# A depthwise convolution woven into a matmul stream: the last far products behind the next gate, one reduce for the cached tokens, low parts and mean later

## The chip, the core and the metric

The kernel runs on one core of a Trainium2 chip. Its engines work side by side, each through its own queue in order: TensorE (PE in the rows, PEld for its weight loads), VectorE (DVE), ScalarE (ACT), GpSimd (POOL) and SyncE (SP), which issues the DMAs here. Semaphores tie them together. The metric is the device time in microseconds, the median of several runs.

## What is computed

One inference step of a two-layer decoder trunk, for 256 new positions of one prompt and 8 sampled tokens (264 columns together), all in float32. Layer 0 mixes tokens with a Conformer convolution, layer 1 with an HGRN2 recurrence; each layer ends in a convolutional feed-forward net. The change lies in the Conformer convolution:

```python
h = x @ w_pw1 + b_pw1
a, gt = jnp.split(h, 2, axis=-1)
u = a * jax.nn.sigmoid(gt)
c, new_buf = causal_depthwise_conv(u, buf, w_dw, b_dw)
c = jax.nn.silu(layernorm(c, ln_g, ln_b))
return c @ w_pw2 + b_pw2, new_buf
```

D_MODEL and D_CONV are 2048, CONV_WIDTH is 31: each channel is convolved with 31 taps over time. For the sampled tokens the 30 older inputs come from a cached state.

## The kernel before

Channels lie on the 128 partitions, so x and every 2048-channel tensor are 16 tiles of 128 x 264. Weights are read in tiles of 128 output channels (1 MB each); one such tile is one *slot* (`slot`), 16 k-steps on TensorE. A weight tile is used in one of two ways (`step`): *native* float32, one matmul per k-step (L184), or *split* into a high part (a cast on ScalarE, L145, `wh`) and a low part (a subtraction on VectorE, L157, `wl`), three matmuls per k-step (L187 to L189), which then also need the activations' high and low parts (`high_parts`, `low_parts`, L275 for the low ones).

The order of work is written out by hand. `slot` first emits the matmuls of its weight tile and then takes its *turn*: three lists of functions, *first*, *early* and *late*, with the casts of coming weights between the first two and their subtractions between the last two. `later(n, f)` puts f into the n-th turn from now. Each engine works through what has been emitted for it in that order.

In the first convolution slots alternate: slot 2i makes a's channel tile i, slot 2i+1 its gate tile. The first 16 and three gate tiles are native, the gate tiles of i >= 3 split. The work on tile i is put into the turns of slots 2i+2 and 2i+3:

- `sigmoid` (L387, ScalarE), then `glu` (L395, VectorE), which makes the tile's gated input `u`; a copy of its end (`ulast`, L397).
- `begin_sums`: ScalarE starts two sums in PSUM, `even` (L413) and `odd` (L414), and one in SBUF, `far` (L419, from the negative of a mean m0; for the first two tiles GpSimd sets it to zero).
- `taps`: 15 instructions on VectorE (L404) that add one tap each to `even` or `odd`.
- `products`: the 14 far taps, in seven pairs. ScalarE multiplies (L435, into `two` for the first pair and `more` for the others, two buffers of `more`), GpSimd adds each pair into `two` (L437) and at the end both halves of `two` into `far` (L443).
- `end_sums`: VectorE adds even and far (L454), the sampled tokens (L455) and odd (L457) into `c`. It stands at the head of the next tile's turn, behind that tile's gate and ahead of its taps.
- `square` and `summed`: running sums of c and its square for the layer norm (L367 on ScalarE, four instructions at L380 on VectorE: `dq` in PSUM, `dsum` and `qsum` for the 8 tokens in SBUF).

For the last tile (15) 13 of the taps are matmuls with diagonal matrices (`diagonals`, L468 on ScalarE; `diagonal_taps`, L474). `centre` takes the column mean of tile 0's c by a matmul with ones (L479), ScalarE scales it into m0 (L481), and it is subtracted from all later sums, so that the squares lose less precision; tiles 0 and 1, which come before it, are corrected afterwards (`catch_up`, L486). `conv_state` multiplies the cached inputs by their taps (L347) and sums them over the 30 positions by halving (L352, L355) into `csum`.

PSUM has three banks of the kind `pt` for the weight slots and the mean. A slot's bank is free again when the tile's sigmoid (gate) or `glu` (a) has read it. The mean's bank is free when L481 has read it.

In time: slots 0 to 5 run without split weights; `conv_state` and `high_parts` stand late in the turn of slot 2, `low_parts` early in that of slot 3, `centre` late in that of slot 5, the catch-ups of tiles 0 and 1 in those of slots 6 and 9, `diagonals` late in that of slot 28. Behind the last tile's sums come the layer norm's statistics, the second pointwise convolution, the feed-forward net, the HGRN2 layer and the second feed-forward net.

Of the kernel before, what the change touches and what calls it, by code (L numbers as in the profile page):

```python
# [49 lines left out]
TAPS, TAPS_LAST = (8, 17, CW), (7, 14, 18)  # L50
# [15 lines left out]
def kernel(ctx: ExitStack, tc: tile.TileContext, a: dict):  # L66
# [255 lines left out]
    with ExitStack() as ph:  # L322
# [23 lines left out]
        def conv_state():  # L346
            vec.tensor_tensor(out=cstate, in0=cstate, in1=wall[:, :, : CW - 1].unsqueeze(3).to_broadcast((P, KT, CW - 1, NB)),  # L347
                              op=ALU.mult)
            n = CW - 1
            while n > 1:  # L350
                half = n // 2
                vec.tensor_tensor(out=cstate[:, :, :half, :], in0=cstate[:, :, :half, :],  # L352
                                  in1=cstate[:, :, half : 2 * half, :], op=ALU.add)
                if n % 2:
                    vec.tensor_tensor(out=cstate[:, :, 0, :] if half > 1 else csum, in0=cstate[:, :, 0, :], in1=cstate[:, :, n - 1, :], op=ALU.add)  # L355
                n = half
            vec.tensor_tensor(out=csum, in0=csum, in1=par[:, COL["b_dw"] : COL["b_dw"] + KT].unsqueeze(2).to_broadcast((P, KT, NB)),
                              op=ALU.add)

        c, m = [], {}  # L360
# [8 lines left out]
        def summed(i):  # L369
            sq = m.pop(("sq", i))  # L370
            if i == 0:
                both = ps.tile([P, 2, SEQ], F32, tag="dq", name="dq", bufs=1)
                for r, z in enumerate("dq"):
                    m[z] = both[:, r, :], gp.tile([P, T], F32, tag=z + "sum", name=z + "sum")
            for z, t in zip("dq", (c[i], sq)):
                for own, cols in (m[z][0], slice(0, SEQ)), (m[z][1][:, SEQ:], slice(SEQ, T)):
# [31 lines left out]
        def begin_sums(i):  # L408
            u, last = m[i], i == KT - 1
            odd_from, top, end = TAPS_LAST if last else TAPS  # L410
# [5 lines left out]
            if i < 2:  # L416
# [5 lines left out]
            m["two", i] = gp.tile([P, 2, SEQ - TAPS_LAST[1]], F32, tag="two", name=f"two{i}")[:, :, : SEQ - top]  # L422
# [53 lines left out]
        def centre():  # L476
# [5 lines left out]
            later_tiles = csum[:, 2:, :]  # L482
            vec.tensor_tensor(out=later_tiles, in0=later_tiles, in1=m["m0"][:, SEQ:].unsqueeze(1).to_broadcast((P, KT - 2, NB)), op=ALU.subtract)
# [5 lines left out]
        def collected():  # L489
            for z in "dq":  # L490
                act.copy(m[z][1][:, :SEQ], m[z][0])
                m[z] = m[z][1]
# [15 lines left out]
        def low_parts():  # L508
            xhl[:] = [low(k, xg[k], xhl[k], "xg") for k in range(KT)]
# [4 lines left out]
        later(3, low_parts)  # L514
        for i in range(KT):
# [8 lines left out]
            if 0 < i < KT - 1:  # L524
                later(0, lambda i=i: end_sums(i - 1))
            if i == KT - 1:
                later(0, diagonal_taps)
                later(0, lambda i=i: (products(i, CW), taps(i, CW), end_sums(i), square(i)), last=True)
                continue
            later(0, lambda i=i: products(i, 2), first=True)  # L530
            later(0, lambda i=i: (products(i, 2), taps(i, 8)))
            later(1, lambda i=i: (products(i, CW), taps(i, CW)))
            if i == KT - 2:
                later(1, lambda i=i: (end_sums(i), square(i), summed(i), collected()), last=True)
                continue
            if i < 2:
                later(4 + i, lambda i=i: catch_up(i), last=True)
                later(5 + i, lambda i=i: summed(i))
            else:
                later(3, lambda i=i: square(i), first=True)  # L540
                later(3, lambda i=i: summed(i), last=True)
            if i == 0:
                later(3, centre, last=True)
            if i == KT - 3:
                later(0, diagonals, last=True)
# [646 lines left out]
```

## Time and profile before

| what | value |
|---|---|
| median of 3 runs (lowest to highest) | 2481.79 us (2481.58 to 2483.23) |
| the profiled execution's own time | 2483.45 us |
| its span, first to last instruction | 2481.7 us |
| mean granted TensorE clock | 0.990 |
| TensorE matmul, weight load busy | 2425.1 us (98%), 2381.4 us (96%) |
| VectorE, ScalarE, GpSimd busy | 1725.5 us (70%), 1249.9 us (50%), 160.8 us (6%) |
| first matmul of the first convolution | 7.57 us |
| gate of tile 0, of tile 15 (L395 starts) | 29.93 us, 259.13 us |
| first matmul of the second pointwise convolution | 276.80 us |

A row of the timeline or the chain gives the start in us, the length in us, engine, line, operation, output and inputs, shapes and a count; in brackets stands how long the engine had been idle before it, and what it waited for. A row of waits reads: engine, waiting line, what it waited for, us in total, times, (in some) the longest. A row of the stretches gives its bounds and length, then busy us (and instructions) of PE, PEld, DVE, ACT and POOL, then the granted clock, the DMA engines' busy share and GB/s. A row of the groups gives the line, the operation with shapes, a count, and behind the bar the sum in us and the mean of one in ns. A row of one line's instructions gives the shortest, median and longest length in ns. Lengths of neighbouring instructions of an engine can overlap by a little, so the step from start to start is used where one follows the other.

### The profile page before, as it was taken

How to read it: one execution, taken by the hardware profiler on the slowest of the kernel's cores; microseconds unless marked ns; L12 is line 12 of the kernel's file. 1: busy time of each engine (PE TensorE's matmuls, PEld its weight loads, DVE VectorE, ACT ScalarE, POOL GpSimd, SP SyncE). 2: the span in 40 equal slices, each digit the busy share in tenths (PEclk: the TensorE clock that was granted, in tenths of full speed). 3: DMA queues.
4: the chain of work that ended last, by engine and by line, in shares of the span. 5: the costliest groups of instructions: out<-in, count | busy, mean ns of one | idle time of the engine just before them, and what ended most of it. 6: DMA issues, size and time to landing. Idle time of an engine off the chain costs nothing.

```text
span 2481.7 us, 49276 instructions
## 1 busy us (share of the span) xinstructions
PE 2425.1 (98%) x20910; PEld 2381.4 (96%) x20910; DVE 1725.5 (70%) x2922; ACT 1249.9 (50%) x2112; POOL 160.8 (6%) x132
## 2 busy tenths in 40 slices
PE   7898799999999999999999999999999999999998
PEld 6898699999999999999999999999999999999998
DVE  8888857676566566657877877857767557656655
ACT  4667644444344344445766666544444444434434
POOL 2776100000000000000000000000000000000000
PEclk9999899999999999999999999999999999999999
DMA  7343255555455465455666555555555455455453
GB/s 266 136 161 145 102 189 190 185 174 175 164 204 182 156 207 180 165 178 200 217 214 221 204 203 213 187 196 197 178 187 173 157 207 177 162 199 183 164 179 126
DMA packets 78141, 453.09 MB, mean 183 GB/s; under 512 B 8544, under 2 KB 13024, under 8 KB 39008
## 3 DMA queue, kind: packets, MB, share of 16 engines
q1 hardware_dynamic: 77920, 449.94, 52.4%
q8 instruction: 164, 2.69, 0.4%
q14 instruction: 57, 0.47, 0.0%
HBM read 436.31 MB, written 15.50 MB: 182 GB/s over the span
## 4 chain that ended last, share of the span: by engine, by line
PE 78%; DVE 15%; ACT 4%; POOL 2%; issue 1%; DMA 0%; SPq 0%; POOLq 0%; DVEq 0%; ACTq 0%
PE p_up L189 14%; PE p_up L187 14%; PE p_up L188 14%; PE p_dn L189 7%; PE p_dn L188 7%; PE p_dn L187 7%; DVE R L765 2%; DVE odd L404 1%; DVE even L404 1%; POOL two L437 1%; PE p_ho L187 1%; PE p_ho L188 1%; PE p_ho L189 1%; PE p_pw L184 1%; PE p_pw L187 1%
## 5 line engine op out<-in xcount | busy, mean ns | idle before, releaser
L187 PE MATMUL p_up<-h_ffn,wh_up 128*128 128x264 f32 x2816 | 801.1, 284 | 0.7 <-DVE x L288 0.7
L189 PE MATMUL p_up<-h_ffn,wl_up 128*128 128x264 f32 x2816 | 800.7, 284 | 0.0
L188 PE MATMUL p_up<-l_ffn,wh_up 128*128 128x264 f32 x2816 | 797.6, 283 | 0.0
L145 ACT CAST wh_up<-w_up 128x2048 fp32r<-128x2048 f32 x176 | 335.9, 1909 | 506.7 <-PE p_up L188 446.7
L157 DVE TENSOR_TENSOR wl_up<-w_up,wh_up 128x2048 fp32r<-128x2048 f32 x176 | 403.6, 2293 | 231.9 <-ACT wh_up L145 231.9
L187 PEld LDWEIGHTS p_up<-h_ffn,wh_up 128*128 128x128 f32 x2816 | 530.1, 188 | 0.9 <-issue 0.9
L189 PEld LDWEIGHTS p_up<-h_ffn,wl_up 128*128 128x128 f32 x2816 | 530.1, 188 | 0.0
L188 PEld LDWEIGHTS p_up<-l_ffn,wh_up 128*128 128x128 f32 x2816 | 529.6, 188 | 0.1
L189 PE MATMUL p_dn<-gh,wl_dn 128*128 128x264 f32 x1408 | 400.8, 285 | 0.0
L187 PE MATMUL p_dn<-gh,wh_dn 128*128 128x264 f32 x1408 | 400.3, 284 | 0.0
L188 PE MATMUL p_dn<-gl,wh_dn 128*128 128x264 f32 x1408 | 400.1, 284 | 0.0
L145 ACT CAST wh_dn<-w_dn 128x1408 fp32r<-128x1408 f32 x128 | 175.8, 1373 | 326.0 <-PE p_dn L188 243.9
L157 DVE TENSOR_TENSOR wl_dn<-w_dn,wh_dn 128x1408 fp32r<-128x1408 f32 x128 | 208.1, 1626 | 108.1 <-ACT wh_dn L145 108.1
L188 PEld LDWEIGHTS p_dn<-gl,wh_dn 128*128 128x128 f32 x1408 | 265.3, 188 | 0.0
L189 PEld LDWEIGHTS p_dn<-gh,wl_dn 128*128 128x128 f32 x1408 | 264.7, 188 | 0.0
L187 PEld LDWEIGHTS p_dn<-gh,wh_dn 128*128 128x128 f32 x1408 | 264.6, 188 | 0.0
L631 DVE SCALAR_TENSOR_TENSOR C<-H,par,C 128x255 f32<-128x255 f32 x352 | 169.3, 481 | 6.3
L437 POOL TENSOR_TENSOR two<-two,more 128x478 f32<-128x478 f32 (+1 forms) x91 | 139.1, 1528 | 101.6 <-ACT more L435 96.7
L184 PE MATMUL p_pw<-xg,w_pw 128*128 128x264 f32 x544 | 125.9, 392 | 9.3 <-ACT m L481 9.3
L286 DVE TENSOR_TENSOR x<-x,p_dn 128x264 f32<-128x264 f32 x128 | 54.9, 429 | 111.9 <-PE p_dn L189 111.9
L184 PEld LDWEIGHTS p_pw<-xg,w_pw 128*128 128x128 f32 x544 | 104.2, 193 | 27.6 <-ACT m L481 10.0
L625 DVE TENSOR_TENSOR H<-p_up,rstd_ffn 128x264 f32<-128x264 f32 x176 | 76.1, 433 | 78.1 <-PE p_up L189 78.1
(339 smaller groups left out, 4525.9 us busy)
## 6 DMA issues: line engine op xcount, KB each, us to landing
w_up<-in_up SPq DMA_DIRECT2D x176, 1024.0 KB
w_dn<-in_dn SPq DMA_DIRECT2D x128, 704.0 KB
w_pw<-in_pw SPq DMA_DIRECT2D x47, 1024.0 KB
w_hf<-in_hf SPq DMA_DIRECT2D x16, 1024.0 KB
w_hq<-in_hq SPq DMA_DIRECT2D x16, 1024.0 KB
w_hi<-in_hi SPq DMA_DIRECT2D x16, 1024.0 KB
w_hg<-in_hg SPq DMA_DIRECT2D x16, 1024.0 KB
w_ho<-in_ho SPq DMA_DIRECT2D x16, 1024.0 KB
```

The costliest lines, as they stand in the source:

```text
L145: act.copy(wh[:, :kk, :], raw[key][:, :kk, :])
L157: vec.tensor_tensor(out=wl[:, :kk, :], in0=raw.pop(key)[:, :kk, :], in1=wh.bitcast(F32)[:, :kk, :], op=ALU.subtract)
L184: pe.matmul(pt[:, :T], wh[:, k, :], full[k], start=(k == 0), stop=last)
L187: pe.matmul(pt[:, :T], wh[:, k, :], rh, start=(k == 0), stop=False)
L188: pe.matmul(pt[:, :T], wh[:, k, :], rl, start=False, stop=False)
L189: pe.matmul(pt[:, :T], wl[:, k, :], rh, start=False, stop=last)
L286: vec.tensor_tensor(out=x[n], in0=x[n], in1=pt[:, :T], op=ALU.add)
L404: vec.scalar_tensor_tensor(out=dst[:, d - first : SEQ - first], in0=m[i][:, : SEQ - d], scalar=weight(i, d), in1=dst[:, d - first : SEQ - ...
L437: pool.tensor_tensor(out=two[:, : hi - lo, :], in0=two[:, : hi - lo, :], in1=out[:, : hi - lo, :], op=ALU.add)
L625: vec.tensor_tensor(out=h, in0=pt[:, :T], in1=rstd, op=ALU.mult)
L631: vec.scalar_tensor_tensor(out=cc[:, d:SEQ], in0=h[:, : SEQ - d], scalar=wv[:, j, 2 - d : 3 - d], in1=cc[:, d:SEQ], op0=ALU.mult, op1=ALU.add)
L765: vec.tensor_tensor(out=new, in0=old, op=ALU.mult, in1=g.rearrange("p r n s -> p r (n s)").unsqueeze(3).to_broadcast((P, 2, 2 * n, b)))
```

## The change

- The seven pairs of products of a tile are dealt out as 2 + 1 in the first of its two turns, 3 in the second, and the last one (with GpSimd's adds into `far`) right behind the next tile's `glu` and `begin_sums`. `two` gets a second buffer.
- `end_sums` of a tile moves from ahead of the next tile's taps to behind them, in the second of its turns.
- `conv_state` sums over the 30 positions with one `tensor_reduce` whose input is seen through a permuted view (the innermost step is 8 elements, 32 bytes).
- `low_parts` is cut in two halves, late in the turns of slots 5 and 6.
- The mean comes later: `NM = 3` tiles start without it, `centre` stands late in the turn of slot 7, with `diagonals` behind it; three catch-ups follow in the turns of slots 8 to 10, their running sums one turn later each. From tile 3 on `square` and `summed` come two tiles later.
- Tile 14 gets its own division (`TAPS_NEXT`): 19 taps on VectorE and five pairs of products.
- `collected`, the copies of the running sums out of PSUM, stands behind tile 15's `begin_sums`.

```diff
-TAPS, TAPS_LAST = (8, 17, CW), (7, 14, 18)
+TAPS, TAPS_NEXT, TAPS_LAST = (8, 17, CW), (10, 21, CW), (7, 14, 18)
...
-            n = CW - 1
-            while n > 1:
-                half = n // 2
-                vec.tensor_tensor(out=cstate[:, :, :half, :], in0=cstate[:, :, :half, :],
-                                  in1=cstate[:, :, half : 2 * half, :], op=ALU.add)
-                if n % 2:
-                    vec.tensor_tensor(out=cstate[:, :, 0, :] if half > 1 else csum, in0=cstate[:, :, 0, :], in1=cstate[:, :, n - 1, :], op=ALU.add)
-                n = half
+            vec.tensor_reduce(out=csum, in_=cstate.rearrange("p k j b -> p k b j"), axis=AX.X, op=ALU.add)
...
+        NM = 3
...
-            odd_from, top, end = TAPS_LAST if last else TAPS
+            odd_from, top, end = TAPS_LAST if last else TAPS_NEXT if i == KT - 2 else TAPS
...
-            if i < 2:
+            if i < NM:
                 pool.memset(far, 0.0)
...
-            m["two", i] = gp.tile([P, 2, SEQ - TAPS_LAST[1]], F32, tag="two", name=f"two{i}")[:, :, : SEQ - top]
+            m["two", i] = gp.tile([P, 2, SEQ - TAPS_LAST[1]], F32, tag="two", name=f"two{i}", bufs=2)[:, :, : SEQ - top]
...
-            later_tiles = csum[:, 2:, :]
+            later_tiles = csum[:, NM:, :]
...
         def collected():
             for z in "dq":
-                act.copy(m[z][1][:, :SEQ], m[z][0])
-                m[z] = m[z][1]
+                own = gp.tile([P, T], F32, tag="sg", name=z + "all", bufs=2)
+                act.copy(own[:, :SEQ], m[z][0])
+                act.copy(own[:, SEQ:], m[z][1])
+                m[z] = own
...
-        def low_parts():
-            xhl[:] = [low(k, xg[k], xhl[k], "xg") for k in range(KT)]
+        def low_parts(half):
+            for k in range(half * KT // 2, (half + 1) * KT // 2):
+                xhl[k] = low(k, xg[k], xhl[k], "xg")
...
-        later(3, low_parts)
+        later(5, lambda: low_parts(0), last=True)
+        later(6, lambda: low_parts(1), last=True)
...
-            if 0 < i < KT - 1:
-                later(0, lambda i=i: end_sums(i - 1))
             if i == KT - 1:
+                later(0, collected, first=True)
                 later(0, diagonal_taps)
...
+            if i > 0:
+                later(0, lambda i=i: products(i - 1, CW), first=True)
+            if i >= NM + 2:
+                later(0, lambda i=i: square(i - 2), first=True)
+                later(0, lambda i=i: summed(i - 2), last=True)
             later(0, lambda i=i: products(i, 2), first=True)
-            later(0, lambda i=i: (products(i, 2), taps(i, 8)))
-            later(1, lambda i=i: (products(i, CW), taps(i, CW)))
+            later(0, lambda i=i: (products(i, 1), taps(i, 8)))
+            later(1, lambda i=i: (products(i, 3), taps(i, CW)))
+            if i > 0:
+                later(1, lambda i=i: end_sums(i - 1))
             if i == KT - 2:
-                later(1, lambda i=i: (end_sums(i), square(i), summed(i), collected()), last=True)
-                continue
-            if i < 2:
-                later(4 + i, lambda i=i: catch_up(i), last=True)
-                later(5 + i, lambda i=i: summed(i))
-            else:
-                later(3, lambda i=i: square(i), first=True)
-                later(3, lambda i=i: summed(i), last=True)
-            if i == 0:
-                later(3, centre, last=True)
-            if i == KT - 3:
-                later(0, diagonals, last=True)
+                later(1, lambda i=i: (end_sums(i), square(i - 1), square(i), summed(i - 1), summed(i)), last=True)
+            if i == NM - 1:
+                later(1, centre, last=True)
+                later(1, diagonals, last=True)
+            if i == NM:
+                for j in range(NM):
+                    later(j, lambda j=j: catch_up(j), last=True)
+                    later(j + 1, lambda j=j: summed(j))
```

More of the change, by code (lines that the diff above doesn't have):

```diff
@@ L373, in summed @@
                 for r, z in enumerate("dq"):
-                    m[z] = both[:, r, :], gp.tile([P, T], F32, tag=z + "sum", name=z + "sum")
+                    m[z] = both[:, r, :], gp.tile([P, NB], F32, tag=z + "sum", name=z + "sum")
             for z, t in zip("dq", (c[i], sq)):
-                for own, cols in (m[z][0], slice(0, SEQ)), (m[z][1][:, SEQ:], slice(SEQ, T)):
+                for own, cols in (m[z][0], slice(0, SEQ)), (m[z][1], slice(SEQ, T)):
                     if i == 0:
@@ L481, in centre @@
             act.mul(m["m0"], pm[:, :T], 1.0 / P)
-            later_tiles = csum[:, 2:, :]
-            vec.tensor_tensor(out=later_tiles, in0=later_tiles, in1=m["m0"][:, SEQ:].unsqueeze(1).to_broadcast((P, KT - 2, NB)), op=ALU.subtract)
+            later_tiles = csum[:, NM:, :]
+            vec.tensor_tensor(out=later_tiles, in0=later_tiles, in1=m["m0"][:, SEQ:].unsqueeze(1).to_broadcast((P, KT - NM, NB)), op=ALU.subtract)
         def catch_up(j):
```

## The prediction

> **What bounds the kernel now.** I read the page's slices first (TensorE is least busy in the first tenth of the span), then who VectorE and TensorE waited for in the first convolution, then busy time by stretch, then one tile's instructions in order of time. The stretch that matters reaches from tile 0's gate (`u`, L395, at 29.93 us) to tile 15's, at 259.13 us: only behind that can the last sums be made, and what follows is the same in both kernels.
>
> ```profile
> 29.93:259.13 229.20, 200.28 (x1149) 179.48 (x1147) 191.52 (x387) 150.33 (x343) 157.63 (x121) 0.94 0.42 147
> DVE c L454 <- POOL far L443: 27.0, 13, 2.3
> DVE u L395 <- ACT sg L387: 3.6, 3, 2.4
> DVE wl_pw L157 <- ACT wh_pw L145: 3.1, 1, 3.1
> DVE csum L483 <- ACT m L481: 2.3, 1, 2.3
> DVE even L404 <- ACT even L413: 0.8, 1, 0.8
> ```
>
> The first row is the stretch: 229.20 us long, TensorE busy 200.28, weight load 179.48, VectorE 191.52, ScalarE 150.33, GpSimd 157.63. TensorE has 29 us of gaps, so it isn't the bound. VectorE idles 229.20 - 191.52 = 37.7 us; the rows under it name 36.8 of them, and 27.0 are one kind: the sum of a tile's parts (L454) waits for GpSimd's `far`. One tile on VectorE shows where:
>
> ```profile
> 126.63 0.49 DVE L395 SCALAR_TENSOR_TENSOR u<-p_pw,par,sg 128x264 f32<-128x264 f32 x1
> 129.36 0.43 DVE L454 TENSOR_TENSOR c<-even,far 128x256 f32<-128x256 f32 x1 [2.24 <-POOL far L443]
> 130.17 0.48 DVE L404 SCALAR_TENSOR_TENSOR even<-u,par,even 128x255 f32<-128x255 f32 x1
> 136.04 2.29 DVE L157 TENSOR_TENSOR wl_pw<-w_pw,wh_pw 128x2048 fp32r<-128x2048 f32 x1
> 138.24 0.43 DVE L380 TENSOR_TENSOR dq<-dq,c 128x256 f32<-128x256 f32 x1
> 138.57 0.83 DVE L380 TENSOR_TENSOR dsum<-dsum,c 128x8 f32<-128x8 f32 x1
> 140.69 0.49 DVE L395 SCALAR_TENSOR_TENSOR u<-p_pw,par,sg 128x264 f32<-128x264 f32 x1
> ```
>
> From gate to gate 14.06 us: 2.73 to L454 (2.24 of it idle), 0.81 for the three sums, 5.87 for 15 taps (0.39 each), 2.20 for the weights' low part, 2.45 for the running sums. TensorE needs less for a pair of weight tiles, as its native tiles show:
>
> ```profile
> 84.86 7.28 PE L184 MATMUL p_pw<-xg,w_pw 128*128 128x264 f32 x32
> 97.83 7.28 PE L184 MATMUL p_pw<-xg,w_pw 128*128 128x264 f32 x32
> PE p_pw L184 <- ACT m L481: 9.3, 1, 9.3
> PE pm L479 <- DVE c L457: 5.1, 1, 5.1
> ```
>
> That is 12.97 us. VectorE loses 1.09 us a pair on it; the three PSUM banks of `pt` absorb that for a while, and TensorE then waits too. The last two rows are the early gap: the matmul of the mean (L479) needs tile 0's sums and holds the third bank until ScalarE has read it (L481). So the sum is made on VectorE's chain, with TensorE as a floor.
>
> **The change part by part.**
>
> *The far products behind the gate.* ScalarE's seventh pair of products, GpSimd's last add and its two adds into `far` move behind the next tile's gate, and `end_sums` of a tile moves behind the next tile's 15 taps. With that L454 no longer stands right behind the gate. In order on ScalarE after gate `u(i)`: copy, `even`, `odd`, `far`, the pair; by
>
> ```profile
> 127.28 0.56 ACT L413 ACTIVATE even<-u,par 128x256 f32<-128x256 f32 x1
> 128.18 0.40 ACT L419 ACTIVATE far<-m 128x256 f32<-128x256 f32 x1
> 131.16 3.83 POOL L437 TENSOR_TENSOR two<-two,more 128x478 f32<-128x478 f32 x3 [1.83 <-ACT more L435]
> 127.95 1.38 POOL L443 TENSOR_TENSOR far<-far,two 128x239 f32<-128x239 f32 x2
> ```
>
> the initial `far` ends 1.95 us after the gate; two products (some 0.8, the length of an 0.88 pair less overlap), one add (3.83/3 = 1.28) and 1.38 for two adds put `far(i-1)` at 5.4 us. VectorE gets to L454 after 1.25 + 5.87 + 2.45 = 9.6 us. The wait goes: **-27.0**. What is late next: the first tap now stands right behind the gate and needs ScalarE's `even`. The trace has that order twice, at tile 0 and at tile 15:
>
> ```profile
> 259.13 0.49 DVE L395 SCALAR_TENSOR_TENSOR u<-p_pw,par,sg 128x264 f32<-128x264 f32 x1 [1.03 <-ACT sg L387]
> 260.38 0.49 DVE L404 SCALAR_TENSOR_TENSOR even<-u,par,even 128x255 f32<-128x255 f32 x1 [0.76 <-ACT even L413]
> ```
>
> Tiles 1 to 14 pay the 0.76: **+10.6**. Behind that waiting tap are queued only its own tile's instructions. A pair is then 14.06 - 2.73 + 1.25 = 12.58 us on VectorE. Does ScalarE come round in time? Its next sigmoid follows the sixth pair, which follows GpSimd's third add of the tile: 5.4 + 3 x 1.28 = 9.3, a pair 0.8, the sigmoid 0.46: 10.5 us after the gate. Yes, by 2 us. The second buffer of `two` lets its products start without waiting for `far`.
>
> *One reduce instead of a tree.*
>
> ```profile
> 34.27 4.15 DVE L347 TENSOR_TENSOR cstate<-cstate,par 128x3840 f32<-128x3840 f32 x1
> 38.45 5.06 DVE L352 TENSOR_TENSOR cstate<-cstate 128x1920 f32<-128x1920 f32 x2
> ...
> 48.95 0.29 DVE L357 TENSOR_TENSOR csum<-csum,par 128x128 f32<-128x128 f32 x1
> 49.16 5.58 DVE L275 TENSOR_TENSOR l_xg<-xg,h_xg 128x264 fp32r<-128x264 f32 x16
> L847 DVE TENSOR_REDUCE wd<-pl 128x64 f32<-128x384 f32 x16 | 8.9, 557 | 0.6
> L761 DVE TENSOR_TENSOR G<-G 128x128 f32<-128x128 f32 x16 | 6.3, 394 | 0.0
> L761 DVE TENSOR_TENSOR G<-G 128x64 f32<-128x64 f32 x16 | 4.3, 268 | 0.0
> ```
>
> The tree fills 48.95 - 38.45 = 10.5 us. The reduce reads 3840 elements whose neighbours are 32 bytes apart. Low end: at the rate of L347, 4.2 us; the one reduce of the trace, L847, strided too but from PSUM, has that rate (557 ns for 384). High end: SBUF operands in steps, L761, where 64 more elements cost 126 ns, 1.97 ns each: 7.7 us. I take 7.7, since that row reads SBUF: **-2.8** (low end -6.3; nothing only if it took the tree's 10.5). The Trainium skill, page "SBUF — State Buffer", section "Door 1: The DMA port swizzle", says that SBUF works in 16-byte lines and that each access that crosses to a new line pays a penalty, without its size; by it the reduce is the slow one, and L761 (8-byte steps) points the same way while L847 can't test it. By full rate the forecast below would be 3.5 us lower.
>
> *Low parts later, in two halves.* The same 16 instructions (5.58 us with GpSimd idle), now in the turns of slots 5 and 6, beside GpSimd's adds. What such company costs, and a catch-up:
>
> ```profile
> L380 DVE TENSOR_TENSOR dsum<-dsum,c x14: 150/830/1190, 97.7 to 257.4; 128x8 f32<-128x8 f32 x14
> L486 DVE TENSOR_TENSOR c<-c,m 128x264 f32<-128x264 f32 x2 | 2.2, 1076 | 0.0
> ```
>
> Eight elements take 0.15 us alone and 0.83 as the median, so a clash costs 0.7. Between none and some seven clashes (GpSimd's adds runnable in the two stretches): 0 to +5, taken **+3**. TensorE first needs them in slot 7; its stall there doesn't reach VectorE's chain, because the three banks let TensorE run most of a pair ahead of the gates.
>
> *Mean later (NM = 3).* One catch-up more, **+1.1** (1076 ns); the subtraction from `csum` shrinks. `pm` now waits for nothing, as tile 0's sums are two slots old, but it still takes the third bank until L481 is done. Behind L481 ScalarE now makes the 13 diagonals, before tile 3's sigmoid:
>
> ```profile
> 231.81 3.89 ACT L468 ACTIVATE diag<-cst,par 128x128 f32<-128x128 f32 x13
> 68.86 0.37 ACT L481 ACTIVATE m<-pm 128x264 f32<-128x264 f32 x1
> ```
>
> The waits at 68 (2.3, for the mean) and at 234 (3.1, weights behind the diagonals) go, **-5.4**; I keep the 3.6 at sigmoids for tile 3's, held by the 3.89, and add **+1.2** for tile 4's, queued behind a square that needs a catch-up late in VectorE's turn.
>
> *Tile 14.* `TAPS_NEXT` gives it 19 taps, 4 x 0.39 = **+1.5**, and two pairs fewer, so its `far` comes before its sums. Two running sums then stand beside an idle GpSimd, where at the old end one did; the other is spared two clashes of 0.7: **-1.4**. `collected` goes behind tile 15's start on ScalarE: two copies of 0.37 delay its products and so its `far`, hidden under the diagonal taps, for which VectorE waited longer at the old end:
>
> ```profile
> 267.96 0.41 DVE L459 TENSOR_TENSOR c<-p_taps,c 128x238 f32<-128x238 f32 x1 [1.60 <-PE p_taps L474]
> ```
>
> *Loads.* No DMA is added or moved, but a split weight tile's buffer comes free with VectorE's low part, and the next gate now comes right behind that. ScalarE's cast of the next weights stands 5.5 us behind the gate (1.95, then four pairs less overlap and a square):
>
> ```profile
> 139.00:140.00 1.00, 1.00 (x6) 0.87 (x5) 1.00 (x3) 0.59 (x2) 0.92 (x2) 1.00 0.75 115
> 142.00:143.00 1.00, 1.00 (x7) 0.84 (x6) 0.00 (x0) 0.65 (x2) 0.91 (x2) 1.00 0.45 188
> ```
>
> After the low part that ended at 138.24 the transfer ran from 139 to 142.5, 4.3 us in all. Still hidden, by 1 us; without that cover each pair would lose what is over 5.5.
>
> *Sum*: -27.0 + 10.6 - 2.8 + 3.0 + 1.1 - 5.4 + 1.2 + 1.5 - 1.4 = **-19.2 us**. The profiled execution took 2483.45 us (span 2481.7 in it), so 2464.3; the median of the runs is 1.66 below it, so **2462.6**.
>
> **The rivals.**
>
> *TensorE becomes the bound.* If the reduce runs at full rate and clashes are few, the pairs of 12.58 us catch up with 12.97. Slot 8 began at 84.86, held by VectorE and L481; ahead of it fall away 6.3 (reduce), 2.3 (mean) and two waits for `far` of 27.0/13 = 2.1, against two taps of 0.76: 73.6. 73.6 + 12 x 12.97 + 1 (sigmoid and gate) = 230.2 for tile 15's gate, 28.9 earlier: 2453. That is the floor.
>
> *ScalarE's ring takes over.* For: in the pair shown the old sigmoid ended just as VectorE came to the gate, because L157 held GpSimd's adds (5.60 us for three, row below). If L157's 2.2 us and 0.5 for a running sum fall ahead of the third add, the sigmoid ends at 13.2 instead of 10.5: 12 x 0.6 = 7 us less gain, 2470. Against: L157 stands behind that add now.
>
> *GpSimd becomes the bound, slower.* Its adds are 1.28 us each, but beside the state's arithmetic six took
>
> ```profile
> 33.20 14.12 POOL L437 TENSOR_TENSOR two<-two,more 128x478 f32<-128x478 f32 x6 [31.99 <-ACT more L435]
> 136.34 5.60 POOL L437 TENSOR_TENSOR two<-two,more 128x478 f32<-128x478 f32 x3 [1.36 <-ACT more L435]
> ```
>
> 2.35 each (first row). If the new places of VectorE's SBUF instructions did that all along, GpSimd would need 6 x 2.35 + 1.38 = 15.5 us a tile, and 12 x (15.5 - 14.06) = 17 us come on top: 2499. It decides from 2.1 us an add. Against: in the tile shown it needed 3.83 + 5.60 + 1.38 = 10.8 us, holds included.
>
> *Nothing gained*: the idle moves from L454 to the first tap and the sigmoids in full, 2482. For it nothing but that the old rings are nearly level.
>
> **How the numbers follow.** Forecast 0.66 (2462.6, own range 2457 to 2468); TensorE's floor 0.16 (2453); ScalarE's ring 0.10 (2470); nothing gained 0.04; GpSimd 0.04. The range reaches from under the floor, 2452, to 2472, which takes in the ring and 2 more for uncertain clashes. A measurement of this kernel can tell 0.2%, 5 us, from no change. All of the first three cases lie below that: faster 0.92, same 0.04, slower 0.04.
>
> **What would show it.** Right: L454 without a wait on `far`; 14 waits of some 0.8 at the first tap; gates 12.6 to 13 us apart; the reduce near 7.7 us; the gap before tile 3's first matmul gone, one before slot 8, for L481; tile 15's gate near 240. Wrong: gates still 14 apart with another releaser, adds on GpSimd over 2 us, a reduce far from both ends, or ScalarE waiting for weights to land.

## The result, and the profile after

The changed kernel took 2464.73 us (median of 4 runs, 2463.86 to 2465.87); before, 2481.68 us in the runs beside it (4 runs, 2480.88 to 2483.23). The ratio is 0.9931, with a 95% interval of 0.9914 to 0.9948: 16.95 us less, where 19.2 were forecast (2462.6). The profiled execution took 2464.92 us, its span 2463.1. Medians here and below are of all executions of a kernel, ratios of the fast ones alone: the medians of the rest alone and of one buffer of `two` each hold one slow execution (4794.87 and 2619.64 us). Line numbers behind the reduce shift by 6: the gate `u` is L389 now, the taps are L398, the sum of a tile's parts L448 and L449.

The stretch from tile 0's gate to tile 15's, by the windows of the changed kernel (bounds, length, then busy time of TensorE, weight load, VectorE, ScalarE, GpSimd, granted clock, DMA share, GB/s):

```profile
29.29:241.52 212.23, 200.24 (x1149) 179.44 (x1147) 198.14 (x385) 146.54 (x336) 152.19 (x120) 0.96 0.45 159
```

It fell from 229.20 to 212.23 us, by 16.97: that is the gain. Both stretches are of one profiled execution each. VectorE's idle time in it fell from 37.7 to 212.23 - 198.14 = 14.1 us, by 23.6; its busy time rose from 191.52 to 198.14, by 6.6. What is left of the idle time, by the waits of VectorE in the same stretch (us in total, times, the longest):

```profile
DVE even L398 <- ACT even L407: 10.6, 14, 0.8
DVE u L389 <- ACT sg L381: 1.8, 3, 0.9
DVE c L448 <- POOL far L437: 1.1, 1, 1.1
```

The wait for `far` went from 27.0 us in 13 places to 1.1 in one (tile 14's), and the first tap's wait for `even` took its place, 14 times 0.76. One pair on VectorE's timeline (start, length, engine, line):

```profile
150.61 0.48 DVE L389 SCALAR_TENSOR_TENSOR u<-p_pw,par,sg 128x264 f32<-128x264 f32 x1
151.85 0.49 DVE L398 SCALAR_TENSOR_TENSOR even<-u,par,even 128x255 f32<-128x255 f32 x1 [0.76 <-ACT even L407]
154.94 0.43 DVE L374 TENSOR_TENSOR dq<-dq,c 128x256 f32<-128x256 f32 x1
155.27 0.24 DVE L374 TENSOR_TENSOR dsum<-dsum,c 128x8 f32<-128x8 f32 x1
155.81 0.39 DVE L374 TENSOR_TENSOR qsum<-qsum,sq_ln 128x8 f32<-128x8 f32 x1
156.12 0.47 DVE L398 SCALAR_TENSOR_TENSOR even<-u,par,even 128x251 f32<-128x251 f32 x1
158.91 0.42 DVE L448 TENSOR_TENSOR c<-even,far 128x256 f32<-128x256 f32 x1
159.24 0.75 DVE L449 SCALAR_TENSOR_TENSOR c<-u,par,csum 128x8 f32<-128x8 f32 x1
160.24 3.15 DVE L157 TENSOR_TENSOR wl_pw<-w_pw,wh_pw 128x2048 fp32r<-128x2048 f32 x1
163.32 0.48 DVE L389 SCALAR_TENSOR_TENSOR u<-p_pw,par,sg 128x264 f32<-128x264 f32 x1
```

Gate to gate is 12.7 us (14.06 before). The sums of tile i-2 now stand between the taps (154.94 to 156.12, 1.18 us instead of 2.45), L448 has no wait, and L449 and the weights' low part L157 take longer than before. The groups of VectorE in that stretch (busy us, mean ns, idle time in front), of the kernel before:

```profile
L157 DVE TENSOR_TENSOR wl_pw<-w_pw,wh_pw 128x2048 fp32r<-128x2048 f32 x13 | 29.8, 2292 | 3.1 <-ACT wh_pw L145 3.1
L380 DVE TENSOR_TENSOR qsum<-qsum,sq_ln 128x8 f32<-128x8 f32 x14 | 12.7, 909 | 0.0
L380 DVE TENSOR_TENSOR dsum<-dsum,c 128x8 f32<-128x8 f32 x14 | 10.6, 759 | 0.0
L275 DVE TENSOR_TENSOR l_xg<-xg,h_xg 128x264 fp32r<-128x264 f32 x16 | 5.6, 426 | 0.0
L455 DVE SCALAR_TENSOR_TENSOR c<-u,par,csum 128x8 f32<-128x8 f32 x15 | 3.3, 218 | 0.0
```

and of the changed one:

```profile
L157 DVE TENSOR_TENSOR wl_pw<-w_pw,wh_pw 128x2048 fp32r<-128x2048 f32 x13 | 39.3, 3021 | 0.0
L275 DVE TENSOR_TENSOR l_xg<-xg,h_xg 128x264 fp32r<-128x264 f32 x16 | 13.2, 894 | 0.0
L449 DVE SCALAR_TENSOR_TENSOR c<-u,par,csum 128x8 f32<-128x8 f32 x15 | 8.9, 594 | 0.0
L349 DVE TENSOR_REDUCE csum<-cstate 128x128 f32<-128x3840 f32 x1 | 7.2, 7176 | 0.0
L374 DVE TENSOR_TENSOR qsum<-qsum,sq_ln 128x8 f32<-128x8 f32 x14 | 5.0, 357 | 0.0
L374 DVE TENSOR_TENSOR dsum<-dsum,c 128x8 f32<-128x8 f32 x14 | 2.9, 208 | 0.0
L480 DVE TENSOR_TENSOR c<-c,m 128x264 f32<-128x264 f32 x3 | 3.0, 1003 | 0.0
```

Two things are to be seen. The small running sums lost 15.4 us (12.7 + 10.6 to 5.0 + 2.9), but L157 and L449 gained 9.5 + 5.6 = 15.1: the company of GpSimd's adds changed its victims. The same kernel bears this out: the low part at 79.99, where GpSimd was idle (its adds ended at 75.86 and started again at 86.03), took 2.28 us instead of 3.15, and the L449 ahead of it 0.22 instead of 0.75. Another, at 93.94, took 2.28 us too, but three adds beside it took 5.81 us, where the next tile's three took 3.75: there the adds paid, as they do in the kernel before. And the low parts of the activations (L275) went from 5.6 to 13.2 us for the same 16 instructions; that is the largest cost that the forecast did not have.

On TensorE, its waits for the low parts (us in total, times, the longest), its timeline around the new stall, and slot 8's native tile behind the mean:

```profile
PE p_pw L188 <- DVE l_xg L275: 6.6, 8, 4.0
68.65 0.45 PE L188 MATMUL p_pw<-l_xg,wh_pw 128*128 128x264 f32 x1 [3.95 <-DVE l_xg L275]
79.03 9.08 PE L184 MATMUL p_pw<-xg,w_pw 128*128 128x264 f32 x32 [0.48 <-ACT m L475]
```

The wait of 9.3 us for the mean's bank has become 0.5, but TensorE now waits in slot 7 for the late low parts, 6.6 us in all and 3.95 at the longest. In the window from the end of that wait to slot 8 the granted clock is 0.51, and slot 8's 32 matmuls, which follow, take 9.08 us instead of 7.28:

```profile
68.65:79.03 10.38, 8.25 (x26) 5.79 (x26) 10.35 (x14) 4.74 (x9) 6.89 (x6) 0.51 0.00 0
```

The kernel before has such a stretch too, behind its wait for the mean (0.50 from 60 to 72 us), so the low clock moved and isn't a new loss as a whole: over the whole stretch the mean granted clock rose from 0.94 to 0.96.

The gates of tiles 3 and 15 stand at 83.2 and 241.5 us (85.6 and 259.1 before). Ahead of gate 3 the chain gained 1.8 us (55.65 to 53.88 since gate 0), behind it 15.2 (173.55 to 158.35).

### The profile page after: what moved, and what is told of

Same layout as the page of the kernel before. It is cut to its first block, busy times and chain, and to the rows that moved or that the text cites. A ratio compares the mean times of both kernels' runs of the same rounds, so it can differ in the third digit from the quotient of the medians.

```text
span 2463.1 us, 49277 instructions
## 1 busy us (share of the span) xinstructions
PE 2422.6 (98%) x20910; PEld 2379.2 (97%) x20910; DVE 1732.1 (70%) x2921; ACT 1246.8 (51%) x2109; POOL 155.4 (6%) x131
## 4 chain that ended last, share of the span: by engine, by line
PE 85%; DVE 12%; ACT 2%; issue 1%; DMA 0%; POOL 0%; SPq 0%; DVEq 0%; ACTq 0%
PE p_up L189 14%; PE p_up L187 14%; PE p_up L188 14%; PE p_dn L189 7%; PE p_dn L188 7%; PE p_dn L187 7%; DVE odd L398 2%; DVE even L398 2%; DVE wl_pw L157 1%; PE p_ho L187 1%; PE p_ho L188 1%; PE p_ho L189 1%; PE p_pw L188 1%; PE p_pw L189 1%; PE p_pw L187 1%; PE p_pw L184 1%
## 5 line engine op out<-in xcount | busy, mean ns | idle before, releaser
L157 DVE TENSOR_TENSOR wl_up<-w_up,wh_up 128x2048 fp32r<-128x2048 f32 x176 | 403.6, 2293 | 231.8 <-ACT wh_up L145 231.8
L157 DVE TENSOR_TENSOR wl_dn<-w_dn,wh_dn 128x1408 fp32r<-128x1408 f32 x128 | 208.1, 1626 | 108.4 <-ACT wh_dn L145 108.4
L431 POOL TENSOR_TENSOR two<-two,more 128x478 f32<-128x478 f32 (+2 forms) x89 | 133.7, 1502 | 90.1 <-ACT more L429 85.7
```

The lines of the kernel that those rows point to most:

```text
L157: vec.tensor_tensor(out=wl[:, :kk, :], in0=raw.pop(key)[:, :kk, :], in1=wh.bitcast(F32)[:, :kk, :], op=ALU.subtract)
L431: pool.tensor_tensor(out=two[:, : hi - lo, :], in0=two[:, : hi - lo, :], in1=out[:, : hi - lo, :], op=ALU.add)
```

## The experiments

Theory A is the prediction's: the gain is the wait for `far`, taken off VectorE's chain, and what is missing of it are the low parts, which stand beside GpSimd's adds now. Theory B says that the rest (the mean and the diagonals in other places, the reduce) carries the gain and the far products little. Smaller rivals are named with their runs. The kernel before was run again beside the experiments: its median was 2483.0 us beside the far products alone, the rest alone, the low parts early and the tree; 2481.88 beside the adds left out, the reduce in memory order and the two with the sums of tile i-2 first; 2482.51 beside the diagonals, the one buffer and the sums of tile i-3. Differences of 1 to 2 us between runs of different groups are therefore within the noise of their times, and there the traces have to decide. Gates are starts of L389 (or the line that stands for it).

**The far products alone.** Tree, mean, diagonals, low parts and tile 14's taps as before; the second buffer of `two`, the far products, `end_sums`, the running sums two tiles later and the place of `collected` as in the change.

```diff
 (edits to the changed kernel)
...
-            vec.tensor_reduce(out=csum, in_=cstate.rearrange("p k j b -> p k b j"), axis=AX.X, op=ALU.add)
+            (the tree of before)
...
-        NM = 3
+        NM = 2
...
-            odd_from, top, end = TAPS_LAST if last else TAPS_NEXT if i == KT - 2 else TAPS
+            odd_from, top, end = TAPS_LAST if last else TAPS
...
-        later(5, lambda: low_parts(0), last=True)
-        later(6, lambda: low_parts(1), last=True)
+        later(3, lambda: (low_parts(0), low_parts(1)))
...
-            later(1, lambda i=i: (products(i, 3), taps(i, CW)))
+            later(1, lambda i=i: (products(i, CW if i == KT - 2 else 3), taps(i, CW)))
...
+            (catch_up, centre and diagonals in the places of before)
```

> The kernel before with one part of the change: the last pair of products and end_sums behind the next gate, two buffers of two, running sums two tiles later, collected behind tile 15's start. The tree, the early low parts, the mean after tile 0, the diagonals at slot 28 and tile 14's taps stay as before. Theory A (VectorE's chain from gate to gate is what counts): no wait for far, some 0.76 us at each first tap, gates 12.6 to 12.7 us apart from tile 5 on. Ahead of tile 3 little is won, since the mean's matmul now waits even longer for tile 0's sums (they stand behind tile 1's taps) and TensorE idles there. About 14 us of the 17 remain: 2467 us (2463 to 2471). Theory B (the gain is the gap that TensorE lost by the later mean): the gap stays or grows, so 2478 to 2488.

Measured: 2468.2 us, ratio 0.9942 [0.9928, 0.9955]: -14.8. Added to the kernel before, this edit alone gives most of the gain, as A said. Two details of A were wrong. One wait for `far` is left, 5.0 us at tile 14. And from tile 7 on the gates are not 12.6 to 12.7 apart but 12.97, TensorE's own pace. Its waits show why, and who waits for it:

```profile
ACT sg L388 <- PE p_pw L189: 21.9, 10, 3.3
PE pm L480 <- DVE c L458: 10.2, 1, 10.2
```

With the mean still asked for early, TensorE loses 10.2 us to it and then has none in hand; ScalarE's sigmoids wait for TensorE. No run has the later mean alone, so what it is worth by itself stays open.

**The rest alone.** The far products, `end_sums` and the single `two` of before; everything else as in the change, the running sums two tiles later too.

```diff
-            m["two", i] = gp.tile([P, 2, SEQ - TAPS_LAST[1]], F32, tag="two", name=f"two{i}", bufs=2)[:, :, : SEQ - top]
+            m["two", i] = gp.tile([P, 2, SEQ - TAPS_LAST[1]], F32, tag="two", name=f"two{i}")[:, :, : SEQ - top]
...
             if i > 0:
-                later(0, lambda i=i: products(i - 1, CW), first=True)
+                later(0, lambda i=i: end_sums(i - 1))
...
-            later(0, lambda i=i: (products(i, 1), taps(i, 8)))
-            later(1, lambda i=i: (products(i, 3), taps(i, CW)))
-            if i > 0:
-                later(1, lambda i=i: end_sums(i - 1))
+            later(0, lambda i=i: (products(i, 2), taps(i, 8)))
+            later(1, lambda i=i: (products(i, CW), taps(i, CW)))
```

> The changed kernel without that part: all of a tile's products and GpSimd's adds in its own two turns, end_sums ahead of the next tile's taps, one buffer of two; reduce, halved low parts, later mean, tile 14's taps stay. Theory A: the waits for far come back (25.9 us more), the 14 waits at the first tap go (10.6 less): 15 us slower than the changed kernel, 2480 us (2476 to 2485). Theory B: it keeps the closed gap, 2464 to 2469.

Measured: 2472.52 us, ratio 0.9959 [0.9943, 0.9974]: -10.5, between the two expectations. Its steps are 13.86 us with the old wait still there, and the groups of VectorE show what else paid:

```profile
L448 DVE TENSOR_TENSOR c<-even,far 128x256 f32<-128x256 f32 x15 | 6.3, 422 | 23.0 <-POOL far L437 23.0
L374 DVE TENSOR_TENSOR qsum<-qsum,sq_ln 128x8 f32<-128x8 f32 x14 | 9.4, 674 | 0.0
L374 DVE TENSOR_TENSOR dsum<-dsum,c 128x8 f32<-128x8 f32 x14 | 2.9, 205 | 0.0
```

The sums of tile i-2 in mid-tile cost 11 us less than at the tile's end (9.4 + 2.9 against 12.7 + 10.6), of which L157 takes 6.9 back (36.7 us busy instead of 29.8); and with the diagonals made early, the step to tile 14 is 13.85 instead of 17.30. The two halves overlap: 14.8 + 10.5 is more than the 17 to 18 that they give together. By the stretch from gate 0 to gate 15 (229.20 us before, 214.93 with the far products alone, 220.26 with the rest alone, 212.23 with both) the far products are worth 14.3 us added first and 8.0 added last. One part of the overlap can be read off: both runs have the later running sums. In the rest alone these, L157 and L449 together fall by 4.1 us (56.4 to 52.3); with the far products behind the gate they don't (56.9 there, 56.1 in the changed kernel), since L157 and L449 then pay for it. B as stated falls, for A's half alone gives most; but A had left this half too small.

**The low parts where they were.**

```diff
-        later(5, lambda: low_parts(0), last=True)
-        later(6, lambda: low_parts(1), last=True)
+        later(3, lambda: (low_parts(0), low_parts(1)))
```

> The changed kernel with all 16 low parts in the turn of slot 3, ahead of its taps, where the kernel before had them. Theory A: the two halves took 4.8 + 8.3 = 13.1 us beside GpSimd's adds; in the old place GpSimd has nothing to do and they take 5.6. VectorE's chain gets shorter by 6 to 7.5 us, and TensorE's waits of 6.6 us for them in slot 7 and the half clock behind them go: 2458 us (2456 to 2460). Rival C (the later place is needed): tile 1's gate comes 5.6 us later, TensorE waits for its bank in slot 6, and the gain is eaten: 2463 to 2467.

Measured: 2461.22 us, ratio 0.9914 [0.99, 0.9927], 3.5 us under the changed kernel. Gate 15 is at 237.1 instead of 241.5. From the source view and the timeline of VectorE:

```profile
L275 DVE TENSOR_TENSOR l_xg<-xg,h_xg x16: 425/426/427, 45.5 to 50.7; 128x264 fp32r<-128x264 f32 x16
76.00 1.26 DVE L477 TENSOR_TENSOR csum<-csum,m 128x104 f32<-128x104 f32 x1
79.31 0.49 DVE L389 SCALAR_TENSOR_TENSOR u<-p_pw,par,sg 128x264 f32<-128x264 f32 x1 [2.06 <-ACT sg L381]
```

All 16 take 425 to 427 ns there (5.6 us), so 7.5 us go; some 3 come back before tile 3, where VectorE now waits 2.06 us for a sigmoid (0.7 in the changed kernel) and L477 takes 1.26 (0.26). Deferring the low parts cost, it did not help. The price is between what A and its rival gave, and C's waits are there: TensorE waits 1.04 us for tile 1's gate in slot 6 and 2.35 for a sigmoid in slot 7, behind which the granted clock was 0.50 from 64 to 68 us. So the low clock, which A had going, stays in part.

**Whether GpSimd is what makes the low parts slow.** GpSimd's adds of `more` into `two` for tiles 1 and 2 are left out, so that those two tiles keep only the first pair of their far taps.

```diff
-                if lo > top:
+                if lo > top and i not in (1, 2):
```

> The changed kernel without GpSimd's adds of more into two for tiles 1 and 2 (that part of their far products is left out; ScalarE still makes them). Theory A: the low parts took 4.8 + 8.3 us because each clashes with one of those adds; without them the first half takes 2.8 us and the second 2.8 to 4.2 (two adds into far are left). Tile 3's gate, at 83.2 us, comes 5 to 6 us earlier. Rival E (the low parts are slow in that place for another reason, TensorE's or the DMAs' reads say): they keep 4.8 and 8.3 us.

One execution took 2460.06 us. The timeline of VectorE, the two halves of the low parts; first of the changed kernel, then of this one:

```profile
59.02 4.85 DVE L275 TENSOR_TENSOR l_xg<-xg,h_xg 128x264 fp32r<-128x264 f32 x8
68.11 8.38 DVE L275 TENSOR_TENSOR l_xg<-xg,h_xg 128x264 fp32r<-128x264 f32 x8
```

```profile
59.25 3.24 DVE L275 TENSOR_TENSOR l_xg<-xg,h_xg 128x264 fp32r<-128x264 f32 x8
66.74 2.83 DVE L275 TENSOR_TENSOR l_xg<-xg,h_xg 128x264 fp32r<-128x264 f32 x8
```

From 13.2 us to 6.1, with nothing changed on VectorE: the cause is shown. In the changed kernel five of those adds ran from 69.03 to 75.86, which is where the second half stands; the first half met adds only up to 61.5. The Trainium skill, page "SBUF — State Buffer", section "Who interferes with whom", says that a VectorE instruction with two SBUF inputs contends with a GpSimd instruction that reads SBUF; this pair of runs agrees and gives the size, 1.05 us (8.38/8) instead of 0.35 (2.83/8) for each in the second half.

**The tree in place of the reduce.**

```diff
-            vec.tensor_reduce(out=csum, in_=cstate.rearrange("p k j b -> p k b j"), axis=AX.X, op=ALU.add)
+            (the tree of before)
```

> The changed kernel with the old tree of adds in place of the reduce. Theory A: the tree took 10.5 us beside GpSimd, the reduce 7.2; all of it lies on VectorE's chain, so 3.3 us slower, 2468 us (2466.5 to 2469.5). Rival D (the end is set by TensorE from slot 8 on, which waits for the low parts' second half anyway): under 1 us.

Measured: 2465.93 us, ratio 0.9935 [0.9922, 0.9947], 1.2 over the changed kernel, less than A's 3 or so and within the two intervals, so the trace decides. The timeline of VectorE:

```profile
37.79 5.05 DVE L352 TENSOR_TENSOR cstate<-cstate 128x1920 f32<-128x1920 f32 x2
45.62 0.29 DVE L355 TENSOR_TENSOR cstate<-cstate 128x128 f32<-128x128 f32 x1
46.60 0.29 DVE L357 TENSOR_TENSOR csum<-csum,par 128x128 f32<-128x128 f32 x1
```

The tree needs 46.60 - 37.79 = 8.8 us here, not the 10.5 of before: a tile's last add and those into `far` come behind the next gate in the new order, so GpSimd is through at 45.1 us (48.8 before), and the tree's last additions stand alone. So the reduce at 7.2 is worth 1.6 us on the chain: the step from gate 0 to gate 1 grows from 18.73 to 20.34 us, and the delay stays until gate 15 (243.1 instead of 241.5). That is half of A's 3.3, and D's TensorE doesn't hide it.

**Why the reduce takes 7.2 us.** Here it reads as many elements in the order of memory, and so sums other groups of 30.

```diff
-            vec.tensor_reduce(out=csum, in_=cstate.rearrange("p k j b -> p k b j"), axis=AX.X, op=ALU.add)
+            flat = cstate.rearrange("p k j b -> p k (j b)").rearrange("p k (b j) -> p k b j", b=NB)
+            vec.tensor_reduce(out=csum, in_=flat, axis=AX.X, op=ALU.add)
```

> The changed kernel with the reduce reading the same 3840 elements in memory order (so that it sums other groups of 30 than it should; a look at its length alone). Theory F (steps of 32 bytes cost): L349 took 7.2 us, now 4.2 us, the rate of the product of the same size ahead of it. Rival G (this reduce from SBUF has that rate in any order): 7.2 us.

One execution took 2462.49 us. The source view of the reduce in this kernel, and then in the changed one (shortest, median and longest in ns):

```profile
L350 DVE TENSOR_REDUCE csum<-cstate x1: 4153/4153/4153, 37.8 to 37.8; 128x128 f32<-128x3840 f32 x1
```

```profile
L349 DVE TENSOR_REDUCE csum<-cstate x1: 7176/7176/7176, 37.8 to 37.8; 128x128 f32<-128x3840 f32 x1
```

Neighbours 32 bytes apart cost 3.0 us: 1.87 ns an element instead of 1.08. The Trainium skill, page "SBUF — State Buffer", section "Door 1: The DMA port swizzle", says that each access that crosses to a new 16-byte line pays a penalty; the two rows agree. The 0.79 ns an element between them are not the price of one crossing, since the reduce in memory order crosses lines too, only less often. Of the two ends in the prediction, the SBUF row was the right one.

**The diagonals where they were.**

```diff
-                later(1, diagonals, last=True)
+            if i == KT - 3:
+                later(0, diagonals, last=True)
```

> The changed kernel with the 13 diagonals at their old place, late in the turn of slot 28. Theory A: in the kernel before they cost 3.1 us there (the weights' cast behind them, VectorE waiting). In the changed order ScalarE idles 2.6 us before each gate, which takes up part of their 3.9 us: tile 13's step grows by 1.3 to 3 us, tile 3's gate comes 0.7 earlier; 2466 us (2465 to 2467.5). Rival: all of it is covered, 2464.

Measured: 2465.94 us, ratio 0.9936 [0.9922, 0.9949], 1.2 over the changed kernel, as expected but within the two intervals. The wait for weights is back, in VectorE's waits:

```profile
DVE wl_pw L157 <- ACT wh_pw L145: 1.8, 1, 1.8
```

The step to tile 14 grows from 12.69 to 15.64 us, for tile 14's gate now waits 2.37 us for its sigmoid as well, and gate 3 comes 0.9 us earlier (82.3).

**One buffer of `two`.** All else as changed.

```diff
-            m["two", i] = gp.tile([P, 2, SEQ - TAPS_LAST[1]], F32, tag="two", name=f"two{i}", bufs=2)[:, :, : SEQ - top]
+            m["two", i] = gp.tile([P, 2, SEQ - TAPS_LAST[1]], F32, tag="two", name=f"two{i}")[:, :, : SEQ - top]
```

> The changed kernel with one buffer of two, so that ScalarE's first pair of a tile waits for GpSimd's adds of the tile before. Theory A: it waits some 2.4 us (the adds end 5.3 us behind the gate, ScalarE is there at 2.9), which its idle 2.6 us before the next gate takes up: same time within 1 us. If GpSimd's ring closes instead, the step from gate to gate grows by up to 1 us, 2465 to 2475.

Measured: 2485.96 us, ratio 1.0014 [1.0005, 1.0024]: 21 us over the changed kernel, a little slower than the kernel before (the interval lies above 1), and far from what was expected. Its waits, ScalarE's and VectorE's:

```profile
ACT two L429 <- POOL far L437: 37.6, 14, 3.4
ACT more L429 <- POOL two L431: 23.4, 16, 2.0
DVE u L389 <- ACT sg L381: 23.2, 11, 2.4
```

and ScalarE's last products and sigmoid in a pair:

```profile
157.07 0.88 ACT L429 ACTIVATE more<-u,par 128x239 f32<-128x239 f32 x2 [1.86 <-POOL two L431]
157.86 0.46 ACT L381 ACTIVATE sg<-p_pw,par 128x264 f32<-128x264 f32 x1
```

A tile's first pair overwrites the `two` that GpSimd reads for the tile before until 5.6 us after the gate (143.86 to 149.42). ScalarE works in order, so all its products come some 2.7 us later (37.6 over 14), and the sigmoid behind them starts 14.0 us after the gate (143.86 to 157.86), where it took 10.2 in the changed kernel (150.61 to 160.79). The pairs take 14.49 us, and VectorE waits 2.37 at most gates. This is the ring of the prediction's rival "ScalarE's ring takes over", closed by the missing buffer and not by L157, as that rival had it.

**The running sums ahead of the taps**, to fill the 0.76 us in which the first tap waits.

```diff
                 later(0, lambda i=i: square(i - 2), first=True)
-                later(0, lambda i=i: summed(i - 2), last=True)
+                later(0, lambda i=i: summed(i - 2))
```

> The changed kernel with the running sums of tile i-2 ahead of tile i's first eight taps, where the first tap waits for ScalarE's even. Theory A: they fill the 0.76 us wait, 10 tiles lose about that and a little clash, so VectorE needs 11.5 to 12 us a pair, under TensorE's 12.97. Then TensorE, which starts slot 8 at 79.0 us either way, sets the end: tile 15's gate can come 4 us earlier at most (237.4 for 241.5), 2461 us (2460 to 2463). Rival H (VectorE alone counts, TensorE's floor doesn't hold): 8 us or more, 2457 or less.

Measured: 2476.92 us, ratio 0.9978 [0.9969, 0.9987], 12 over the changed kernel; both theories had it faster. The timeline of VectorE:

```profile
158.16 0.43 DVE L374 TENSOR_TENSOR dq<-dq,sq_ln 128x256 f32<-128x256 f32 x1 [2.18 <-ACT sq_ln L361]
```

The square of tile i-2 stands behind `even`, `odd`, `far` and a pair on ScalarE, so VectorE trades a wait of 0.76 us for one of 2.18. The same edit with the low parts early:

> Both edits: low parts in the turn of slot 3, and the running sums ahead of the taps. With the low parts early slot 8 starts at 75.2 us and slot 10 at 88.2; from there TensorE needs 11 x 12.97 = 142.7, so tile 15's gate can come at 231.9 where it came at 237.1 with the low parts early alone. Theory A with TensorE's floor: 2456 us (2455 to 2458). If the gates are held by ScalarE's ring instead, 2458 to 2461.

Measured: 2472.97 us, ratio 0.9964 [0.9951, 0.9977], steps of 13.94, for the same reason.

**The sums of tile i-3 ahead of the taps**, whose square is a whole tile old, with the low parts early.

```diff
-        later(5, lambda: low_parts(0), last=True)
-        later(6, lambda: low_parts(1), last=True)
+        later(3, lambda: (low_parts(0), low_parts(1)))
...
                 later(0, lambda i=i: square(i - 2), first=True)
-                later(0, lambda i=i: summed(i - 2), last=True)
+                if i > NM + 2:
+                    later(0, lambda i=i: summed(i - 3))
...
-                later(1, lambda i=i: (end_sums(i), square(i - 1), square(i), summed(i - 1), summed(i)), last=True)
+                later(1, lambda i=i: (end_sums(i), square(i - 1), square(i), summed(i - 2), summed(i - 1), summed(i)), last=True)
```

> Low parts in the turn of slot 3, and the running sums of tile i-3 (not i-2) ahead of tile i's taps, so that their square on ScalarE is a tile old. If the 2.2 us wait for the square was all that spoilt the earlier order: no wait at the square, none at the first tap, VectorE needs 10.5 to 12.1 us a pair, TensorE's 12.97 become the step from gate to gate, and its slots from 10 on (88.2 us) set the end: tile 15's gate at 232 to 234, 2457 us (2455.5 to 2459). If VectorE still sets the step, it stays 12.7 and the time that of low parts early alone, 2461.

Measured: 2459.39 us, ratio 0.9908 [0.9895, 0.9922]: the lowest median of all. Its gates come 11.4 to 13.0 us apart from tile 5 to tile 10 and then 12.97, up to tile 14. The waits of ScalarE and TensorE:

```profile
ACT sg L381 <- PE p_pw L189: 11.6, 6, 2.2
PE p_pw L184 <- ACT m L475: 3.9, 1, 3.9
```

Now ScalarE waits for TensorE: this is the floor of the prediction's first rival, reached once VectorE's pair is short enough. Against the low parts early alone it is 1.8 us less, and the two intervals overlap, so that step itself isn't settled; the gates don't show it, for the stretch from gate 0 to gate 15 is as long in both (207.57 and 207.46 us). Tile 15's gate, expected at 232 to 234, stands at 237.4: TensorE waits 3.9 us for the mean's bank, slot 8's matmuls behind that take 10.16 us, and in the step to tile 15 (15.78 us) three tiles' running sums and a wait of 2.43 us for `far` stand ahead of the gate.

## Why the prediction was right, and where a size was off

The mechanism was right: the stretch lost 16.97 us where the steps added up to 19.2. That the sum came so near is in part luck, since the two largest misses (+4.6 and -3.0) have opposite signs. Step by step, on VectorE's chain from gate to gate:

| step | forecast, us | measured, us |
|---|---|---|
| wait for `far` | -27.0 | -25.9 (27.0 to 1.1) |
| first taps wait for `even` | +10.6 | +9.8 (0.8 to 10.6) |
| reduce for tree | -2.8 | -3.3 (10.5 to 7.2) |
| low parts beside GpSimd | +3.0 | +7.6 (5.6 to 13.2) |
| third catch-up | +1.1 | +0.8 (2.2 to 3.0) |
| mean and weights behind diagonals | -5.4 | -5.4 (2.3 and 3.1 gone) |
| waits at sigmoids | +1.2 | -1.8 (3.6 to 1.8) |
| running sums at tile 14 | -1.4 | -0.3 for those of all tiles, with L157 and L449 (56.4 to 56.1) |

Tile 14's four taps were forecast at +1.5; all taps together are busy 1.7 us more. The rows come to -16.8. The 1.1 us that are left of the first row are tile 14's, whose `far` was to come before its sums and came 1.12 us after VectorE was there.

**The term that was mis-sized is the low parts: +3, at most +5, forecast; +7.6 measured.** The count of clashes was taken too low and the halves were treated alike. In fact the first half takes 4.85 us and the second 8.38, in which each of the eight instructions ran against an add. That GpSimd causes it is shown by leaving the adds out (6.1 us); undoing the deferral gives 3.5 us in the time. The step "its stall there doesn't reach VectorE's chain" held but for a remainder. TensorE lost 6.6 us in slot 7 by its waits for `l_xg`; the matmul of the mean, behind slot 7, so started at 77.47 us, ScalarE waited 4.52 us for that and then had the mean, the 13 diagonals and tile 3's sigmoid to do (78.58 to 83.13), and tile 3's gate waited 0.71 us for the sigmoid.

**The sigmoid of tile 3** was to keep a wait of 3.6 us; it kept 0.71. With the low parts early it is 2.06: the late low parts held VectorE itself, so it came to that gate with less to wait for. The two misses, +4.6 and -3.0, belong together in part: with the low parts early 1.35 us of that wait are back, while 1.03 us of the 3.6 had been tile 15's, which fell away.

**A steady pair** was forecast at 12.58 us and took 12.7, but not with the parts that were given. The running sums came to 1.18 instead of 2.45 and L157 to 3.1 instead of 2.20, and the three sums to 1.33 instead of 0.81 (158.91 to 160.24). The prediction kept the old durations in new places; the sum survived because what collides with GpSimd's adds changed but not how much, which the prediction gave no reason for: luck. The order of ScalarE's work was right to 0.1 us, by its timeline:

```profile
211.54 0.46 ACT L381 ACTIVATE sg<-p_pw,par 128x264 f32<-128x264 f32 x1
```

It ends at 212.00, 10.6 us after tile 12's gate at 201.4, where 10.5 was forecast.

**The reduce** was sized from L761 at 7.7 us and took 7.18. L761 has two inputs in 8-byte steps and the reduce one in 32-byte steps, and no run shows that the two are slow for one reason, so the nearness is partly luck. Of the low end, the prediction read too much into L847: 557 ns for 384 elements are 1.45 ns each, and near L347's 1.08 only if some 0.15 us of fixed length (an estimate, from the shortest row of eight elements) is taken off.

**The second buffer** was given one sentence, that products start without waiting. That was true and far under its price: without it the whole gain and 3.5 us more are lost (2485.96 against 2482.51 beside it). The experiment's own expectation made the same mistake.

**The rivals.** TensorE's floor of 2453 asked for slot 8 at 73.6 us; it began at 79.03, for the reduce ran at 7.2 and not 4.2 us and the low parts held slot 7. From there 79.03 + 12 x 12.97 + 1 = 235.7, and 1.8 more for slot 8's slow matmuls, lies 4 us ahead of the gate that was measured, so VectorE stayed the bound. The floor is real, as the kernels with the mean early and with the sums of tile i-3 ahead of the taps show, both at 12.97. ScalarE's ring stayed open by 2 us and closes with one `two`. GpSimd's adds were not the bound: VectorE waited for `far` once.

What stays open: of the 7 to 8 us by which far products and rest overlap, some 3 are the running sums, which gain 4.1 us in the rest alone and next to nothing with the far products behind the gate; the others were followed only as far as TensorE's pace in the one and the old wait in the other. No run shows the later mean or tile 14's taps alone.

## What to carry to other kernels

A wait is removed by moving the waiter behind work that doesn't need it, but price each moved instruction in its new company: of two-input VectorE work beside GpSimd's adds, a third of a microsecond can become one. An instruction that is moved past a gate makes its buffer live past the gate too, so look up who writes that buffer next and what is queued behind the writer; here that one buffer decided between 17 us gained and 3.5 lost. Before a sum is put into an idle gap, look at when its last input is made, since the gap was 0.76 us wide and VectorE then waited 2.18 for the input.

## What the runs showed of the hardware

A reduce over fp32 in SBUF takes 1.08 ns an element in the order of memory and 1.87 with steps of 32 bytes. A VectorE instruction on 264 elements with two SBUF inputs took 0.35 us by itself in a row of eight and 1.05 beside GpSimd's adds; that a whole row of eight slows alike had not been expected. The reduce is no such company. GpSimd's adds on its timeline, three of them beside the reduce in the changed kernel, and the same three beside the tree put back:

```profile
39.16 3.78 POOL L431 TENSOR_TENSOR two<-two,more 128x478 f32<-128x478 f32 x3 [0.32 <-ACT more L429]
```

```profile
39.14 6.03 POOL L438 TENSOR_TENSOR two<-two,more 128x478 f32<-128x478 f32 x3 [0.32 <-ACT more L436]
```

That is 1.26 us an add against 2.0. A wait of 3.95 us on TensorE was followed by 10.38 us at a granted clock of 0.51, and slot 8's 32 matmuls behind it took 9.08 us instead of 7.28; with the sums of tile i-3 ahead of the taps, a wait of 3.89 us was followed by 10.16 us for the same matmuls.
